# A two-layer encoder trunk on one core: products for the second layer's modulation are done later, the last heads' queries are copied at one point, the last head's operands are split in another order, and one query of the second layer is finished later

## The chip, the cores and the metric

The kernel runs on one core of a Trainium2 chip. The core has five engines, each with its own instruction stream that runs in order: TensorE (PE, matrix products), VectorE (DVE), ScalarE (ACT), GpSimd (POOL) and SyncE (SP), which in this kernel issues every DMA transfer. The metric is the device time of one execution in microseconds. One execution of each kernel is also recorded by the hardware profiler, and everything that is read of single instructions comes from that record.

## The reference

The input is a sequence of 1024 positions of width 1024 in float32, one batch. Two layers follow each other and a last RMS norm closes the trunk:

```python
for i in range(DEPTH):                       # DEPTH = 2
    shift, scale, gate = silu(c) @ ada_w[i] + ada_b[i], split in three
    h = rmsnorm(x, norm_g[i]) * (1.0 + scale) + shift
    y = diff_attention(h, ...) if i == 0 else mla(h, ...)
    x = x + gate * y
return rmsnorm(x, final_norm_g)
```

Layer 0 is differential attention with eight heads. One input projection gives q, k, v and z, each 1024 wide. q and k are turned by rotary position embedding (rope) in pieces of 64. For each head two attention maps are formed; the second is multiplied by a learned lambda and taken from the first, and the result meets the values. The head's output is normalised, multiplied by silu(z), and goes through an output projection.

```python
p = softmax(q @ k * scale)                   # two maps per head
p = p[:, :, 0] - lam * p[:, :, 1]
o = rmsnorm(p @ v, subln_g) * (1 - lambda_init) * silu(z)
y = o @ w_out
```

Layer 1 is latent attention: queries, keys and values come from narrow projections (384 and 256 wide). Each of its eight heads has 128 channels without rope, and 64 with it; the rope key is common to all heads.

## The kernel before

**Products.** Every matrix product of two float32 numbers is made of three reduced ones: each operand is split in a high part (a cast to the matrix engine's own float type) and a low part (the operand less its high part), and `mm3` (lines 181 to 184) adds high by high, high by low and low by high. So each tile of weights or activations goes through an ACT cast and a subtraction on DVE or POOL before PE can read it. Names show it: `wvr` is a value weight as loaded, `wvh` and `wvl` are its parts (L524, L533, L534); `wraw`, `wh`, `wl` (L206, L227, L228) are those of the other weights; `woh`, `wol`, `oah`, `oal` (L1177, L1178) those of layer 0's output projection. A matrix instruction is 128 x 128 by 128 x 512.

**Start of layer 0.** The tokens are normalised and transposed in two halves. The weights of the first 512 value channels meet both halves first (`vacc`). After that come the second half of head 0's keys and queries (`gen_half`, "half 1"), and then eight *value tiles* (`v0_tile`, sums in `vps`) for the other 512 channels, one for each 128 tokens. Each value tile ends in `store_v`: ACT casts the sum (L362), DVE subtracts (L363), and SP stores both parts to device memory (`vS`, L365), from where heads load them as `vt` (L374). Three `v_hl` buffers serve six of these stores.

**Modulation of layer 1.** The 2048 numbers of shift and scale of layer 1 are sixteen products of a 128 x 1024 weight with silu(c), each one instruction on DVE (`mod_dot`, L424) that waits for a 512 KB load (`ada<-in_ada_ss`, L419). `gen_mods` hands them out one at a time: seven in the first pass over the second half of the tokens, two in the second half of head 0's keys, two in that of its queries, and five among the value tiles, by the table `MODS`.

**Rope and queries.** For each half of a head's q or k, `rope` copies the sum to `rp_raw` on ACT (L321), swaps channel groups by four small transfers to `rp_sw` (L323), multiplies by cosine (`rp_r`, L324) and sine (L329), and adds both (`fin`, L331 on POOL or L336 on DVE). Then `g` stacks the result: `stack_q` makes two ACT casts (`qa`, L352, L353), two POOL subtractions (`qb`, L354, L355) and four transfers of 128 KB (L357, L358); `stack_k` makes `ks` likewise, with no transfers. These steps stand in a queue, `side`, and one of its entries is run at each tick while PE works at the stream of projections of the next heads; an entry `None` is a tick with nothing to do.

**Attention.** For each tile of 128 queries PE makes the two score maps `s` from `ks` and `qa`, `qb` (L851), DVE takes the maximum (`nm`, L400), ACT the exponential (`e`, L402), DVE combines both maps (L859), PE transposes (`tr`, L383), ACT and DVE split the transpose (`pth`, L385; `ptl`, L386), and PE multiplies it with the values (`pv`). The projections of the next heads (`acc`) and the gate z (`zth` by ACT at L785, `gz` by DVE at L786) are put between.

**Output projection of layer 0.** It is done on 512 x 512 blocks with seven products where the plain way takes eight (a scheme of Strassen's kind). Sums of blocks of the heads' outputs are formed by `combine` (four POOL instructions, L1124 to L1128), the operands are split by `split_a` and `split_w` (L1177, L1178), and the first products are begun during the last head's attention, by the table `PRE0`, with a step number `i` from 0 to 10. A block `k` is one that is kept in place; its loads are at L1313 and L1333.

**Layer 1.** The same order of work: value tiles (`vps`, `v_hl`), rope queries (`qpa`, `qpb`, by the same `stack_q`), score maps at L2003 and so on.

**Order.** Where the code asks for nothing else, a scheduler sets the order on each engine from the order of the code; `in_turn`, `behind` and `tc.issue_after` tie an instruction to a place behind another. Each engine then runs its list strictly in order, and so does SP: a transfer whose source isn't ready holds all that are behind it.

Of the kernel before, what the change touches and what calls it, by code (L numbers as in the profile page):

```python
# [42 lines left out]
SPL1 = 2  # L43
Z_PRE = 16
V_LATE = 6
MODS = (2, 1, 1, 1, 0, 0, 0, 0)
V1_AT = (3, 2)
NORM_AT = 5
PRE0 = (0, 0, 0, 0, 1, 2, 2, 2, 3, 2, 2)
PRE1 = (0, 0, 0, 0, 0, 0, 0, 1, 1, 1, 1)  # L50
LAST1 = (((0, 1), 0, HF), ((2,), 0, HF), ((3,), 0, 256), ((3,), 256, HF))
Z_LAST = 2
# [29 lines left out]
def trunk(ctx: ExitStack, tc: tile.TileContext, A, out):  # L82
# [447 lines left out]
    def split_wv(raw, eng=G):  # L530
        h_ = p1b.tile([P, HF], F32R, name="wvh", tag="wv", bufs=16)
        l_ = p1b.tile([P, HF], F32R, name="wvl", tag="wv", bufs=16)
        S.copy(h_, raw)  # L533
        eng.tensor_sub(l_, raw, f32v(h_))  # L534
        return h_, l_

    psum("ps1", accx=3, tr=1, cb=1)
# [183 lines left out]
    vacc = [bank("acc", "vacc") for _ in range(4)]  # L721
    for k in range(KT + SKEW1):
        if k < KT:
            if k > 0:
                next(mods_g)
            with tc.issue_after(q_split), tc.issue_after(q_mm):
                h_last = h_chunk(0, xs1, k, h0[k][1], p1, V if k in HL_V else G, k % 2 == 1)
        if k >= SKEW1:
            k0 = k - SKEW1
            hh, hl = h0[k0][1]  # L730
            for tt in range(4):
                c_ = slice(tt * P, (tt + 1) * P)
                mm3(vacc[tt], hh[:, c_], hl[:, c_], wv0[k0][0], wv0[k0][1], k0 == 0, k0 == KT - 1)
# [32 lines left out]
    def q_done(h):  # L766
        def f(acc, half):
            rot, fin = rope(wp, acc, half, SC0, *[G if h else V] * 2)

            def g():  # L770
                qa = a0a.tile([P, 2, HF], F32R, name="qa", tag="qs", bufs=4)
                qb = a0a.tile([P, 2, HF], F32R, name="qb", tag="qs", bufs=4)
                stack_q(qa, qb, r.pop() if r else fin())
                QS.setdefault(h, [None, None])[half] = qa, qb

            r = []
            sum_ = [lambda: r.append(fin()), None][: 1 + (h < 5)] if h else []
            side.add(*[None] * ROT, rot, *[None] * (DEF - 1 - ROT), *sum_, g)
        return f

# [23 lines left out]
        k_done(0)(kacc, 0)  # L804
    with tc.issue_after(mod_load.last):
        z0raw = fetch_strip([A["w_s0"][2, 0, f] for f in range(2)], [4, 4])
    for i, _ in enumerate(gen_half(wk0, h0, 1, lambda acc: k_done(0)(acc, 1))):
        if i % 4 == 3:
            next(mods_g)
    wz0 = split_strip(z0raw)  # L810
    q_done(0)(qacc, 0)
    for i, _ in enumerate(gen_half(wq0, h0, 1, lambda acc: q_done(0)(acc, 1))):
        if i % 4 == 3:
            next(mods_g)
    st1.close()
    st2a = ExitStack()
    a0a = pool(st2a, "a0a")
# [15 lines left out]

    pend = [t for t in side.q if t]
    side.q.clear()
    for t in pend[:4]:
        t()
    turn = 0
    stream0.step(Z_PRE)

# [431 lines left out]
    def extra0(i):  # L1272
# [41 lines left out]
        if i == 4:  # L1314
            sv.split_a(0, 0, G)
            both(0, 1)
            sv.split_a(0, 2, G)
        if i == 5:
            sv.split_w(0, 2)
        for n, h in ((), (), (), (), (), ((0, 3),), ((1, 0), (1, 1)), ((1, 2),), (), (), ())[i]:  # L1320
            both(n, h)
        while rests:
# [14 lines left out]
        if i == 8:  # L1337
            sv.split_w(1, 3)
            a11, a12, a21, a22 = k0["pair"]
            for n, t in ((2, a11), (3, a22), (4, a12), (5, a21)):  # L1340
                sv.kept[n][2] = t
            k0["sum"] = combine(*k0["pair"])
        if i > 7:
            next(k0["sum"], None)
        for _ in range(PRE0[i]):
            pre0.step()

# [83 lines left out]
            next(sp)  # L1431

    sv0.split_a(1, 3, G)
    e_last = mk["S"]
    assert pre0.n == 15
    for h in range(4):
# [501 lines left out]

    st5 = ExitStack()
    ap = pool(st5, "attn1")  # L1940
    KN, QN, QP, late_q = {}, {}, {}, []

    def kn_done(h):
        def f(acc, half):
# [14 lines left out]
    def qp_done(h):  # L1959
        def f(acc, half):  # L1960
# [8 lines left out]
            side.add(None, rot, *[None] * DEF1)  # L1969
            if h and half:  # L1970
                late_q.append(g)
            else:
                side.add(g)
        return f
# [92 lines left out]
    ap2 = pool(st5, "attn1b")  # L2067
    stp = ExitStack()
    ap3, nob = pool(stp, "attn1c", side="right"), 8
    for h in range(NH - 1):  # L2070
        attn1(h, lambda i: FILL1[i], lambda i: next(gate1, None))
        while late_q:
            late_q.pop(0)()
        stream1.step(sum(steps1[: h + 2]) - stream1.count)
# [308 lines left out]
```

## Time and profile before

| | |
|---|---|
| three runs, median (lowest to highest) | 1422.78 us (1421.39 to 1426.56) |
| the profiled execution | 1421.18 us |
| its span, first to last instruction | 1419.2 us |
| mean granted TensorE clock | 0.991 |
| busy: PE, DVE, ACT, POOL | 97%, 66%, 52%, 53% |

The profile's page gives, for each engine, the busy time as a share of the span. "Idle" of an instruction is the time its engine stood before it, and the name behind the arrow is what released it. Times inside the span count from its first instruction. An instruction's own length on PE is that of a pipelined product; two products of 512 columns that follow without a wait start 0.23 us apart.

### The profile page before, as it was taken

To read this page: it belongs to the slowest core of one execution; us is meant where nothing else is said; L and a number is where in the kernel's file an instruction comes from. 1 tells how busy PE (TensorE), PEld (TensorE's weight loads), DVE (VectorE), ACT (ScalarE), POOL (GpSimd) and SP (SyncE) were. 2 spreads that over 40 slices of the span, in tenths; PEclk is the share of its full clock that TensorE was granted. 3 is DMA by queue.
4 is the path that set the end of the run, shared out by engine and by line. 5 is a ranking of instruction groups with operands and counts; after the bars stand their busy time and mean duration, and the time that the engine had idled before them with its cause. 6 is when DMAs were issued, how large, how long until landed. Compare 5 with 4: busy or idle time off the path is not lost. (4 is left out here: it accounts for less than half of the span.)

```text
span 1419.2 us, 20732 instructions
## 1 busy us (share of the span) xinstructions
PE 1382.2 (97%) x7350; PEld 1152.0 (81%) x7350; DVE 939.5 (66%) x1339; ACT 736.9 (52%) x1331; POOL 752.1 (53%) x590
## 2 busy tenths in 40 slices
PE   8999999999999999999999999999999999999997
PEld 6777888888888887887787788887888888888886
DVE  8665677777666665668597885645666655555685
ACT  5523465565555655557546443335454454455554
POOL 5415174758686857575694323533141165653783
PEclk8999999999999999999999999999999999999999
DMA  9785734343444434426564136498544354566463
GB/s 344 250 231 182 221 93 134 99 136 98 149 114 154 135 117 120 141 75 193 163 231 163 38 104 216 129 313 223 167 114 129 94 176 171 188 208 209 142 243 119
DMA packets 149066, 231.54 MB, mean 163 GB/s; under 512 B 20577, under 2 KB 57569, under 8 KB 148962
## 3 DMA queue, kind: packets, MB, share of 16 engines
q1 hardware_dynamic: 148962, 230.21, 51.7%
q8 instruction: 58, 0.95, 0.3%
q14 instruction: 46, 0.38, 0.1%
HBM read 144.74 MB, written 61.81 MB: 146 GB/s over the span
## 5 line engine op out<-in xcount | busy, mean ns | idle before, releaser
L385 ACT CAST pth<-tr 128x512 fp32r<-128x512 f32 x256 | 150.1, 586 | 294.4 <-PE tr L383 292.4
L400 DVE TENSOR_REDUCE nm<-s 128x1 f32<-128x1024 f32 x192 | 233.7, 1218 | 90.6 <-PE s L851 78.8
L386 DVE TENSOR_TENSOR ptl<-tr,pth 128x512 fp32r<-128x512 f32 x256 | 176.0, 688 | 146.6 <-ACT pth L385 146.0
L228 POOL TENSOR_TENSOR wl<-wraw,wh 128x512 fp32r<-128x512 f32 (+2 forms) x79 | 101.4, 1285 | 197.8 <-ACT wh L227 166.3
L402 ACT ACTIVATE e<-s,nm 128x1024 f32<-128x1024 f32 x128 | 143.5, 1121 | 32.4 <-DVE nm L400 30.3
L383 PE MATMUL tr<-ident,e 128*128 128x128 f32 x1024 | 156.3, 275 | 3.0 <-DVE ptl L386 2.8
L383 PEld LDWEIGHTS tr<-ident,e 128*128 128x128 f32 x1024 | 122.0, 141 | 45.6 <-DVE ptl L386 21.0
L182 PE MATMUL acc<-h0h,wh 128*128 128x512 f32 x360 | 151.6, 421 | 0.0
L182 PE MATMUL pv<-pth,vt 128*128 128x256 f32 x512 | 147.1, 287 | 0.0
L183 PE MATMUL pv<-ptl,vt 128*128 128x256 f32 x512 | 145.7, 285 | 0.0
L184 PE MATMUL pv<-pth,vt 128*128 128x256 f32 x512 | 144.6, 282 | 0.0
L184 PE MATMUL acc<-h0h,wl 128*128 128x512 f32 x360 | 143.6, 399 | 0.0
L183 PE MATMUL acc<-h0l,wh 128*128 128x512 f32 x360 | 142.7, 396 | 0.0
L324 POOL TENSOR_TENSOR rp_r<-rp_raw,cosT 128x512 f32<-128x512 f32 x38 | 49.7, 1307 | 98.4 <-ACT rp_raw L321 49.8
L183 PEld LDWEIGHTS pv<-ptl,vt 128*128 128x128 f32 x512 | 97.6, 191 | 2.9
L182 PEld LDWEIGHTS pv<-pth,vt 128*128 128x128 f32 x512 | 97.5, 190 | 2.9
L184 PEld LDWEIGHTS pv<-pth,vt 128*128 128x128 f32 x512 | 97.6, 191 | 0.1
L1178 POOL TENSOR_TENSOR wol<-wol,woh 128x512 fp32r<-128x512 f32 x56 | 83.0, 1504 | 21.4 <-ACT woh L1177 18.8
L851 PE MATMUL s<-ks,qa 128*128 128x512 f32 x256 | 83.4, 407 | 6.3 <-DMA qa<-qa 4.5
L329 POOL TENSOR_TENSOR rp_sw<-rp_sw,sinT 128x512 f32<-128x512 f32 x42 | 56.3, 1340 | 52.7 <-DMA rp_sw<-rp_raw 52.1
L859 DVE SCALAR_TENSOR_TENSOR e<-s,z,e 128x1024 f32<-128x1024 f32 x64 | 82.2, 1284 | 2.2
L851 PE MATMUL s<-ks,qb 128*128 128x512 f32 x256 | 81.3, 398 | 0.8 <-DMA qb<-qb 0.8
(412 smaller groups left out, 3488.6 us busy)
## 6 DMA issues: line engine op xcount, KB each, us to landing
ada<-in_ada_ss SPq DMA_DIRECT2D x32, 512.0 KB, 5.6
wraw<-in_w_s SPq DMA_DIRECT2D x64, 256.0 KB, 2.9
vS<-v_hl SPq DMA_DIRECT2D x32, 512.0 KB, 5.8
vt<-vS SPq DMA_DIRECT2D x32, 512.0 KB, 4.8
wol<-tS SPq DMA_DIRECT2D x56, 256.0 KB, 5.0
tS<-ob SPq DMA_DIRECT2D x48, 256.0 KB, 2.0
rp_sw<-rp_raw SPq DMA_DIRECT2D x168, 64.0 KB, 2.0
bc_s<-bc_d SPq DMA_DIRECT2D x34, 256.0 KB, 4.0
```

What stands on the lines that cost most here:

```text
L182: PE.matmul(psum, ah, bh, start=first, stop=False, skip_group_check=skip)
L183: PE.matmul(psum, ah, bl, start=False, stop=False, skip_group_check=skip)
L184: mm3.last = PE.matmul(psum, al, bh, start=False, stop=last, skip_group_check=skip).ins
L228: sub = (V if pair_of else G).tensor_sub(l_[:, :n], raw[:, :n], f32v(h_[:, :n]))
L383: transpose_p.last = PE.transpose(tr[:, j, :], p[:, kt * P : (kt + 1) * P], ident).ins
L385: mk["S"] = S.copy(pth[kh][:, :, dst], tr).ins
L386: mk["V"] = V.tensor_sub(ptl[kh][:, :, dst], tr, f32v(pth[kh][:, :, dst])).ins
L400: mk["V"] = V.reduce_max(nm, s_ps, axis=AX.X, negate=True).ins
L402: mk["S"] = S.activation(e, s_ps, AF.Exp, bias=nm, scale=1.0, accum_out=zs).ins
L851: PE.matmul(s_ps[:, kc * HF : (kc + 1) * HF], src[:, c, ql], KS[h][kc][:, c, :], start=fst, stop=not fst)
L859: combined.append(V.scalar_tensor_tensor(out=e0, in0=e1, scalar=z1[:, 0:1], in1=e0, op0=ALU.mult, op1=ALU.add).ins)
L1178: sub = eng.tensor_sub(lo, raw, f32v(hi))
```

## The change

Four groups of edits, all of them to the order of work; no arithmetic is added or taken away.

1. *Modulation products.* Five of the sixteen `mod_dot` are moved. The first pass does six in place of seven, the second halves of head 0's keys and queries do none in place of four, and the value tiles do ten in place of five (`MODS`). Their loads move with them. The first four waiting tasks of `side` (among them the stacking of head 0's keys) are tied to a place behind the last split of a value weight.
2. *Queries of heads 5, 6 and 7.* The rope sum `fin` and the stacking `g`, which were one tick apart, are now one task, a tick earlier.
3. *Last head.* The split of weight block (0, 2) comes with its activation block, one of the early products moves from step 8 to step 7, and `combine`, which was done in steps 8 and 9, comes after the last split, `split_a(1, 3)`.
4. *Layer 1.* The stacking of the second half of head 0's rope query, which stood before the last value tiles, is done after tile 1 of the first head.

```diff
--- before.py
+++ after.py
@@ -43,10 +43,10 @@
 SPL1 = 2
 Z_PRE = 16
 V_LATE = 6
-MODS = (2, 1, 1, 1, 0, 0, 0, 0)
+MODS = (2, 3, 3, 2, 0, 0, 0, 0)
 V1_AT = (3, 2)
 NORM_AT = 5
-PRE0 = (0, 0, 0, 0, 1, 2, 2, 2, 3, 2, 2)
+PRE0 = (0, 0, 0, 0, 1, 2, 2, 3, 2, 2, 2)
 PRE1 = (0, 0, 0, 0, 0, 0, 0, 1, 1, 1, 1)
 LAST1 = (((0, 1), 0, HF), ((2,), 0, HF), ((3,), 0, 256), ((3,), 256, HF))
 Z_LAST = 2
@@ -531,7 +531,7 @@
         h_ = p1b.tile([P, HF], F32R, name="wvh", tag="wv", bufs=16)
         l_ = p1b.tile([P, HF], F32R, name="wvl", tag="wv", bufs=16)
         S.copy(h_, raw)
-        eng.tensor_sub(l_, raw, f32v(h_))
+        split_wv.last = eng.tensor_sub(l_, raw, f32v(h_)).ins
         return h_, l_
 
     psum("ps1", accx=3, tr=1, cb=1)
@@ -721,7 +721,7 @@
     vacc = [bank("acc", "vacc") for _ in range(4)]
     for k in range(KT + SKEW1):
         if k < KT:
-            if k > 0:
+            if 0 < k < 7:
                 next(mods_g)
             with tc.issue_after(q_split), tc.issue_after(q_mm):
                 h_last = h_chunk(0, xs1, k, h0[k][1], p1, V if k in HL_V else G, k % 2 == 1)
@@ -774,7 +774,7 @@
                 QS.setdefault(h, [None, None])[half] = qa, qb
 
             r = []
-            sum_ = [lambda: r.append(fin()), None][: 1 + (h < 5)] if h else []
+            sum_ = [lambda: r.append(fin()), None] if 0 < h < 5 else []
             side.add(*[None] * ROT, rot, *[None] * (DEF - 1 - ROT), *sum_, g)
         return f
 
@@ -804,14 +804,12 @@
         k_done(0)(kacc, 0)
     with tc.issue_after(mod_load.last):
         z0raw = fetch_strip([A["w_s0"][2, 0, f] for f in range(2)], [4, 4])
-    for i, _ in enumerate(gen_half(wk0, h0, 1, lambda acc: k_done(0)(acc, 1))):
-        if i % 4 == 3:
-            next(mods_g)
+    for _ in gen_half(wk0, h0, 1, lambda acc: k_done(0)(acc, 1)):
+        pass
     wz0 = split_strip(z0raw)
     q_done(0)(qacc, 0)
-    for i, _ in enumerate(gen_half(wq0, h0, 1, lambda acc: q_done(0)(acc, 1))):
-        if i % 4 == 3:
-            next(mods_g)
+    for _ in gen_half(wq0, h0, 1, lambda acc: q_done(0)(acc, 1)):
+        pass
     st1.close()
     st2a = ExitStack()
     a0a = pool(st2a, "a0a")
@@ -833,8 +831,9 @@
 
     pend = [t for t in side.q if t]
     side.q.clear()
-    for t in pend[:4]:
-        t()
+    with tc.issue_after(split_wv.last):
+        for t in pend[:4]:
+            t()
     turn = 0
     stream0.step(Z_PRE)
 
@@ -1314,9 +1313,7 @@
         if i == 4:
             sv.split_a(0, 0, G)
             both(0, 1)
-            sv.split_a(0, 2, G)
-        if i == 5:
-            sv.split_w(0, 2)
+            both(0, 2)
         for n, h in ((), (), (), (), (), ((0, 3),), ((1, 0), (1, 1)), ((1, 2),), (), (), ())[i]:
             both(n, h)
         while rests:
@@ -1339,9 +1336,6 @@
             a11, a12, a21, a22 = k0["pair"]
             for n, t in ((2, a11), (3, a22), (4, a12), (5, a21)):
                 sv.kept[n][2] = t
-            k0["sum"] = combine(*k0["pair"])
-        if i > 7:
-            next(k0["sum"], None)
         for _ in range(PRE0[i]):
             pre0.step()
 
@@ -1431,6 +1425,8 @@
             next(sp)
 
     sv0.split_a(1, 3, G)
+    for _ in combine(*k0["pair"]):
+        pass
     e_last = mk["S"]
     assert pre0.n == 15
     for h in range(4):
@@ -1938,7 +1934,7 @@
 
     st5 = ExitStack()
     ap = pool(st5, "attn1")
-    KN, QN, QP, late_q = {}, {}, {}, []
+    KN, QN, QP, late_q, first_q = {}, {}, {}, [], []
 
     def kn_done(h):
         def f(acc, half):
@@ -1969,6 +1965,8 @@
             side.add(None, rot, *[None] * DEF1)
             if h and half:
                 late_q.append(g)
+            elif half:
+                first_q.append(g)
             else:
                 side.add(g)
         return f
@@ -2067,8 +2065,13 @@
     ap2 = pool(st5, "attn1b")
     stp = ExitStack()
     ap3, nob = pool(stp, "attn1c", side="right"), 8
+    def amid1(i):
+        next(gate1, None)
+        if i and first_q:
+            first_q.pop()()
+
     for h in range(NH - 1):
-        attn1(h, lambda i: FILL1[i], lambda i: next(gate1, None))
+        attn1(h, lambda i: FILL1[i], amid1)
         while late_q:
             late_q.pop(0)()
         stream1.step(sum(steps1[: h + 2]) - stream1.count)
```

What stands where is shown at three places. Line numbers after the change are lower by one to four from L804 to L2066.

The first is DVE, around the last value weight splits (`wvl`) of the start of layer 0; `ISA ada,mod...` is a modulation product, and the row under it reads its sum. Before:

```order
L534 TENSOR_TENSOR wvl<-wvr,wvh 128x512 x2
L424 ISA ada,modb_105<-ada,c_202,vec 128x1024
L424 ISA modb_105 128x1
L324 TENSOR_TENSOR rp_r<-rp_raw,cosT 128x512
L534 TENSOR_TENSOR wvl<-wvr,wvh 128x512 x4
L336 TENSOR_TENSOR rp_r<-rp_r,rp_sw 128x512
L324 TENSOR_TENSOR rp_r<-rp_raw,cosT 128x512
L363 TENSOR_TENSOR v_hl<-vps,v_hl 128x512
L424 ISA ada,moda_104<-ada,c_202,vec 128x1024
```

and after:

```order
L534 TENSOR_TENSOR wvl<-wvr,wvh 128x512 x2
L324 TENSOR_TENSOR rp_r<-rp_raw,cosT 128x512
L534 TENSOR_TENSOR wvl<-wvr,wvh 128x512 x4
L324 TENSOR_TENSOR rp_r<-rp_raw,cosT 128x512
L336 TENSOR_TENSOR rp_r<-rp_r,rp_sw 128x512
L363 TENSOR_TENSOR v_hl<-vps,v_hl 128x512
L324 TENSOR_TENSOR rp_r<-rp_raw,cosT 128x512
L336 TENSOR_TENSOR rp_r<-rp_r,rp_sw 128x512
L324 TENSOR_TENSOR rp_r<-rp_raw,cosT 128x512
L786 SCALAR_TENSOR_TENSOR gz<-zth,acc 128x512
```

The product among the splits and the four behind them are gone from here, and the gate `gz` follows directly; before, it came behind another `v_hl` and the sums for lambda.

The second is SP while PE ends head 5's attention and goes on to head 6, whose first query half is `qa`, `qb`; `rp_sw` belongs to head 6's second query half, and `bc_s` is a row that is spread over all partitions for the normalisation of a finished head. Before:

```order
L408 DMA bc_d<-rq_y 128x4
L206 DMA wraw<-in_w_s 128x512
L323 DMA rp_sw<-rp_raw 32x512 x2
L410 DMA bc_s<-bc_d 128x512
L323 DMA rp_sw<-rp_raw 32x512 x2
L357 DMA qa<-qa 64x512
L358 DMA qa<-qa 64x512
L357 DMA qb<-qb 64x512
L358 DMA qb<-qb 64x512
```

and after:

```order
L408 DMA bc_d<-rq_y 128x4
L357 DMA qa<-qa 64x512
L206 DMA wraw<-in_w_s 128x512
L358 DMA qa<-qa 64x512
L410 DMA bc_s<-bc_d 128x512
L357 DMA qb<-qb 64x512
L358 DMA qb<-qb 64x512
L323 DMA rp_sw<-rp_raw 32x512 x4
```

The two transfers of `qa` now stand ahead of the spread row, those of `qb` right behind it, and the four small ones of `rp_sw` behind them all.

The third is POOL in the last head's attention, where the operands of the output projection are split; `ob<-ob` are the four instructions of `combine`. Before:

```order
L1178 TENSOR_TENSOR wol<-wol,woh 128x512 x2
L1124 TENSOR_TENSOR ob<-ob 128x512
L1125 TENSOR_TENSOR ob<-ob 128x512
L1127 TENSOR_TENSOR ob<-ob 128x512
L1128 TENSOR_TENSOR ob<-ob 128x512
L1178 TENSOR_TENSOR oal<-k_6673,oah 128x512
```

and after:

```order
L1177 TENSOR_TENSOR wol<-wol,woh 128x512 x2
L1177 TENSOR_TENSOR oal<-k_6673,oah 128x512
L1123 TENSOR_TENSOR ob<-ob 128x512
L1124 TENSOR_TENSOR ob<-ob 128x512
L1126 TENSOR_TENSOR ob<-ob 128x512
L1127 TENSOR_TENSOR ob<-ob 128x512
```

The low part `oal` of the kept block is now made ahead of `combine`. In layer 1, on SP, the four transfers of the second rope query half (`qpa`, `qpb`) move behind five stores `vS` and two loads `c2h`; on ACT its two casts move behind all the value tiles' casts.

## The prediction

> **What bounds the kernel now.** I read the page first. It has TensorE busy for nearly the whole span, in 1421.18 us for the profiled execution:
>
> ```profile
> span 1419.2 us, 20732 instructions
> PE 1382.2 (97%) x7350; PEld 1152.0 (81%) x7350; DVE 939.5 (66%) x1339; ACT 736.9 (52%) x1331; POOL 752.1 (53%) x590
> ```
>
> No product is taken away, so only PE's idle time and time at a lowered clock can be won: 37 us of idle. Second I read PE's waits (line waited for, total us, times, longest):
>
> ```profile
> PE s L851 <- DMA qa<-qa: 4.5, 4, 2.3
> PE vps L182 <- DVE v_hl L363: 2.3, 1, 2.3
> PE oy L184 <- POOL oal L1178: 1.7, 2, 1.2
> PE oy L183 <- POOL wol L1178: 1.7, 3, 1.1
> PE vps L182 <- DVE gz L786: 1.5, 1, 1.5
> PE vps L183 <- DVE wvl L534: 1.0, 1, 1.0
> PE s L851 <- DMA qb<-qb: 0.8, 2, 0.5
> ```
>
> Nearly all of them are at places that the change touches. Third, stretches of the span: length, busy us (and count) of PE, PEld, DVE, ACT, POOL, then granted clock, DMA share, GB/s.
>
> ```profile
> 80.00:98.00 18.00, 17.01 (x74) 13.40 (x73) 10.68 (x17) 4.24 (x8) 0.00 (x0) 1.00 0.88 268
> 98.00:108.00 10.00, 8.40 (x28) 5.79 (x27) 6.78 (x8) 3.56 (x6) 4.36 (x4) 0.83 0.90 228
> 114.00:144.00 30.00, 28.52 (x126) 23.23 (x126) 14.19 (x24) 10.90 (x18) 16.69 (x11) 1.00 0.60 182
> 120.00:132.00 12.00, 10.52 (x47) 8.35 (x46) 7.54 (x15) 6.72 (x12) 10.89 (x7) 1.00 0.16 57
> 558.00:566.00 8.00, 5.74 (x24) 4.40 (x23) 2.71 (x4) 0.87 (x2) 4.06 (x3) 0.79 0.42 106
> 676.00:680.00 4.00, 3.40 (x11) 2.78 (x12) 3.04 (x5) 1.62 (x3) 3.99 (x4) 0.64 0.00 0
> 968.00:974.00 6.00, 3.65 (x17) 2.68 (x16) 2.42 (x3) 3.57 (x7) 3.43 (x3) 1.00 0.92 263
> ```
>
> Three of PE's waits are followed by time at a lowered clock (0.83, 0.79, 0.64), so these cost more than the wait itself; the longest, at 969, is not.
>
> **A. Modulation products.** The value tiles stop between 98 and 108: 10.00 less 8.40 is 1.6 us idle, and 10 us at 0.83 lose up to 1.7 us. PE waits there for the splits of the last value weights, whose loads are held back by full DMA queues (share 0.88). Taking one product ahead of them away takes one load of 512 KB away: at the row's 268 GB/s that is 2.0 us of transfer, and its DVE instruction 1.3 us. The loads then come up to 2.0 us earlier; of the 3.3 us that can be won I take 1.3, since the remaining loads keep their own order and buffers. Ends: 0 and 3.0.
>
> The wait for `gz` is a chain that I read in the order of time on ACT and DVE:
>
> ```profile
> 119.47 0.59 ACT L362 CAST v_hl<-vps 128x512 fp32r<-128x512 f32 x1 [8.64 <-PE vps L184]
> 119.96 0.62 ACT L344 CAST ks<-rp_r 64x512 fp32r<-64x512 f32 x1
> 123.41 0.69 DVE L324 TENSOR_TENSOR rp_r<-rp_raw,cosT 128x512 f32<-128x512 f32 x1 [2.62 <-POOL ks L347]
> ```
>
> The key casts stood behind a value tile's cast, POOL's `ks` behind them, DVE's `rp_r` behind that, and `gz` behind `rp_r`. In the new order the casts, `rp_r` and `gz` come ahead of this tile. ACT stood idle for 8.64 us before it, which holds four casts of 0.62, so the 1.5 us go, and 0.1 of refilling: 1.6 (ends 0 and 1.6).
>
> Against it stand five products and five loads in the value tiles. A product is 1.28 us, and up to 2.36:
>
> ```profile
> L424 DVE CUSTOM_DVE_ANT_0 ada<-ada,c,vec x16: 1272/1283/2360, 71.8 to 148.9; 128x1024 f32<-128x1024 f32 x16
> 110.07 2.36 DVE L424 CUSTOM_DVE_ANT_0 ada<-ada,c,vec 128x1024 f32<-128x1024 f32 x1
> 110.06 1.29 POOL L329 TENSOR_TENSOR rp_sw<-rp_sw,sinT 128x512 f32<-128x512 f32 x1 [0.63 <-DMA rp_sw<-rp_raw]
> ```
>
> So DVE gets 6.4 to 11.8 us more. It is idle for 15.8 of the 30 us from 114 to 144 (30 less 14.19), and the DMA engines are nearly empty from 120 to 132 (share 0.16), room for twelve times 0.84 by 268 GB/s, 2.7 MB, where five loads are 2.6 MB. The cover is thin but there. What could break it is SP's order:
>
> ```profile
> SPq L206 <- POOL wl L228: 12.2, 2, 11.0
> ACT v_hl L362 <- DMA vS<-v_hl: 10.7, 2, 5.4
> ```
>
> SP already stands 11 us for a weight buffer with stores `vS` behind it, and ACT then waits twice for a store to land, 10.7 us, while PE's idle time in these 30 us (30 less 28.52) is the 1.5 for `gz` and nothing else. In the new order the first of these stores goes ahead of that stand, so loads may slip by about 5 us unnoticed. I take 0.7 of loss (ends 0 and 3). A comes to 1.3 + 1.6 - 0.7 = 2.2.
>
> [...]
>
> **B. Queries.** In time order, ACT and SP ahead of head 6, PE, and, last, PE at head 7:
>
> ```profile
> 554.18 0.61 ACT L352 CAST qa<-rp_r 64x512 fp32r<-64x512 f32 x1
> 555.29 1.14 SPq L323 DMA_DIRECT2D rp_sw<-rp_raw  x2
> 556.53 0.54 SPq L357 DMA_DIRECT2D qa<-qa  x1
> 560.86 0.58 PE L851 MATMUL s<-ks,qa 128*128 128x512 f32 x1 [2.26 <-DMA qa<-qa]
> 561.66 0.63 PE L182 MATMUL acc<-h0h,wh 128*128 128x512 f32 x1
> 562.09 0.63 PE L183 MATMUL acc<-h0l,wh 128*128 128x512 f32 x1
> 632.59 0.70 PE L851 MATMUL s<-ks,qa 128*128 128x512 f32 x2 [1.20 <-DMA qa<-qa]
> ```
>
> Now the casts come a tick earlier, ahead of an exponential, and `qa` goes out ahead of `bc_s` and `rp_sw`: about 3 us earlier, which covers 2.26. `qb` still stands behind `bc_s`; if it lands 0.3 to 1.3 us late, that is a new, smaller wait. Behind the old wait products start 0.43 us apart (561.66, 562.09) where 0.23 is usual, for some seven of them: 1.3 us. Of 2.3 + 1.3 = 3.6 I take 2.9 (ends 0.9 and 3.6). Of the other waits for `qa` (4.5 less 2.3) and `qb` (0.8), head 7 has 1.2 and heads 4 and 5 share 1.8. Head 4 is not changed; I give head 5 a third, 0.6, which goes. At head 7 the order puts `qa` ahead of only two of four `rp_sw`, at 0.6 us each, but its casts later: 0 (ends -1.2 and 1.2). B: 3.5.
>
> **C. Last head.**
>
> ```profile
> 674.04 1.29 POOL L923 TENSOR_TENSOR o<-o,gz 128x512 f32<-128x512 f32 x1 [3.34 <-ACT o L917]
> 694.26 1.29 POOL L1124 TENSOR_TENSOR ob<-ob 128x512 f32<-128x512 f32 x1
> 699.62 1.26 POOL L1178 TENSOR_TENSOR oal<-k,oah 128x512 fp32r<-128x512 f32 x1
> ```
>
> `wol` of block (0, 2) stood behind the product with `gz`, which waited 3.34 us for ACT; it now goes ahead, and the 1.1 go, with the clock's 0.36 of 4 us behind it (1.4): I take 2.4 (ends 0 and 2.5). `oal` started 5.4 us behind the first `combine` instruction (699.62 less 694.26) and PE waited 1.2 for it; ahead of them it is early by far, and `combine` itself ends one instruction (1.3 us) later, which nothing waits for before the next group: 1.2 (ends 0 and 1.2). One weight load goes out behind five others, and a POOL product of head 7 behind two rope steps: 0.4 of loss, ends 0 and 1.5. C: 3.2.
>
> **D. Layer 1.**
>
> ```profile
> 968.94 0.62 ACT L352 CAST qpa<-rp_r 64x512 fp32r<-64x512 f32 x1 [3.41 <-POOL rp_r L331]
> 970.22 1.07 ACT L362 CAST v_hl<-vps 128x512 fp32r<-128x512 f32 x2
> 987.28 0.63 PE L2003 MATMUL s<-kps,qpa 128*128 128x512 f32 x2
> 978.98 2.32 SPq L1862 DMA_DIRECT2D c2h<-in_c  x2
> DMA to landing us min/median/max: 7.2/7.6/8.0
> ```
>
> ACT stood 3.41 us for POOL's sum with a finished value tile behind it. Without the two casts there PE's 2.3 for `v_hl` go, and 0.2 of refilling: 2.5. New is a late query: its four transfers now follow the `c2h` loads (issued from 979.0, landing in 7.2 to 8.0 us), and PE wants it at 987.28, less the 2.5 won: 984.8. The queue is ahead by as much and by four transfers, so the query lands between 984 and 987: 0.7 of loss (ends 0 and 2.3). D: 1.8.
>
> **Sum.** 2.2 + 3.5 + 3.2 + 1.8 = 10.7. Against the profiled 1421.18 that is 1410.5; the median of the runs is 1.6 above it, so 1412 for the median. All best ends give 1.6 + 3.0 + 0.6 + 3.6 + 1.2 + 2.5 + 1.2 + 2.5 = 16.2, so 1406.6; all worst ends 0 - 3 + 0.9 + 0.6 - 1.2 - 1.5 + 0.2 = -4.0, so 1427, if everything failed at once. What this kernel's measurement can tell from no change is about 0.5%, 7.1 us: the line is at 1415.7, and my forecast 3.7 us beyond it.
>
> The clock is worth 1.3 + 1.3 in this sum. [...]
>
> **Rivals.** *Waits that move.* The late operand is replaced by the next one: `qb` behind `bc_s` at head 6, the value weights at 99, the late query at 985. With A at 0.3, B at 1.5, C at 2.4 and D at 0.5 the gain is 4.7: 1418, no difference. For it speaks that these engines had little to spare (`qa` and `qb` were issued within 2 us of each other); against it, that C and the `gz` wait leave nothing late behind them.
>
> *Slower: SP stands among the value tiles.* SP issues the new loads three at a time ahead of a store `vS`, and there are three buffers, so a third load waits for a product, with stores and queries behind it. Fully in a row, five products in their long form (11.8) and five transfers of 2.0 us (10) are 21.8 us; with the gain of A's rest, B, C and D (11.4, without the 0.7) that gives 1433. It turns the sign once PE waits over 11.4 us there, and shows as slower over 18.5. Against it: 15.8 us of idle DVE, the empty DMA stretch, and no PE wait there now.
>
> *The lowered clock stays.* If the clock falls after whatever short waits remain, at head 6 and in the last head, the 1.3 + 1.3 are not won: 1412 + 2.6 = 1414.7, hardly past the line. That it stayed at 1.00 behind the wait at 969 says that the link is loose.
>
> *The change doesn't do what it says.* "Last heads' queries at once" holds for heads 5 and 6 by the order, for head 7 half; without B's 2.9 the time is 1415, at the line.
>
> **Chances.** Forecast (faster) 0.52; the clock stays 0.08, of it 0.05 faster; B failing, at the line, 0.05, of it 0.03 faster; waits that move, no difference, 0.26; slower by the value tiles 0.09. So faster 0.60, same 0.31, slower 0.09. The range reaches from all best ends, 1406, into the slow rival's beginning, 1424.
>
> **What would show it.** Right: no PE wait for `gz` near 124, none for `qa` near 556, none for `oal` near 697, none for `v_hl` near 967; granted clock 1.00 near 560 and 676; PE's idle sum down from 37 us to about 29. Wrong: new PE waits for `v_hl` or `nm` between 110 and 150, for `qpa` or `qpb` near 985, or for `qb` near 556.

## The result, and the profile after

| | before | changed |
|---|---|---|
| median of six runs each, us | 1421.62 | 1413.83 |
| lowest to highest | 1418.34 to 1426.56 | 1411.87 to 1415.68 |
| profiled execution, its span | 1421.18, 1419.2 | 1415.68, 1414.0 |
| granted clock in the profiled execution | 0.991 | 0.992 |

The ratio is 0.9943, with a 95% interval of 0.9922 to 0.9963: 8 us faster, between 5 and 11. A second series of six runs of the changed kernel (last batch below) has a median of 1411.52 and a ratio of 0.9927 (0.9913 to 0.9942). The prediction said 1412, of 1406 to 1424.

First the page of the changed kernel, then PE's waits (line waited for, total us, times, longest), those that answer to the waits shown before:

```profile
span 1414.0 us, 20751 instructions
PE 1379.2 (98%) x7350; PEld 1150.3 (81%) x7350; DVE 939.8 (66%) x1339; ACT 737.5 (52%) x1331; POOL 752.8 (53%) x590
```

```profile
PE tr L383 <- DVE ptl L386: 5.1, 7, 1.5
PE s L850 <- DVE e L858: 2.7, 5, 1.0
...
PE s L850 <- DMA qa<-qa: 1.8, 2, 1.4
...
PE s L850 <- DMA qb<-qb: 1.5, 2, 0.9
PE vps L182 <- ACT wvh L533: 1.4, 1, 1.4
...
PE vps L183 <- DVE wvl L534: 0.8, 1, 0.8
```

The waits for `gz` (1.5), for `v_hl` in layer 1 (2.3) and the long one for `qa` (2.3) are gone. The two for the value weights are still there, 1.4 and 0.8 where 0.5 and 1.0 stood. The waits for `ptl` and `e`, ACT and DVE inside attention, were there before, 4.5 us together:

```profile
PE tr L383 <- DVE ptl L386: 2.8, 5, 0.9
...
PE s L851 <- DVE e L859: 1.7, 3, 1.0
```

They grew to 7.8. PE's idle time went from 37.0 us to 34.8 (1414.0 less 1379.2); the prediction had named 29 as a sign. So 3.0 of the 5.2 us between the two spans are busy time that got shorter. The mean clock, 0.991 and 0.992, accounts for some 1.4 of that by an estimate (0.001 of 1414); the rest stays open.

Stretches of the changed kernel (length, busy us of PE, PEld, DVE, ACT, POOL, then clock, DMA share, GB/s):

```profile
98.00:108.00 10.00, 8.37 (x22) 6.11 (x23) 4.37 (x6) 5.19 (x9) 7.00 (x6) 0.66 0.45 126
114.00:150.00 36.00, 36.00 (x160) 29.78 (x160) 23.61 (x39) 8.99 (x16) 13.60 (x8) 1.00 0.98 305
555.00:566.00 11.00, 10.46 (x62) 8.80 (x61) 6.60 (x9) 5.29 (x10) 7.11 (x6) 1.00 0.39 107
676.00:684.00 8.00, 7.58 (x49) 6.49 (x48) 7.26 (x11) 6.89 (x13) 5.25 (x6) 1.00 0.49 123
```

With ten products among the value tiles PE does not wait there at all (36.00 of 36), though the DMA engines are full (0.98). The stall at 98 to 108 is as long as before (1.63 us idle, 1.60 before) and at a lower clock, 0.66 where it was 0.83. The clock at head 6 and in the last head is full (1.00 from 555 to 566 and from 676 to 684).

To compare more than two traces I cut the span at instructions that every kernel has: the first product of head 0's second query half (`acc`, near 82), the first maximum `nm` of heads 1, 4 and layer 1's head 2, two `nm` inside heads 5 and 6, the first output product `oy`, the first `oz`, and the first value product `vps` of layer 1 ("layer 1's start"). A time in the next table is the start of one such instruction less that of another, taken from the trace of each kernel.

### The profile page after: what moved, and what is told of

Read it like the earlier page. It is cut to its first block, busy times and chain, and to the rows that moved or that the text cites. A ratio compares the mean times of both kernels' runs of the same rounds, so it can differ in the third digit from the quotient of the medians.

```text
span 1414.0 us, 20751 instructions
## 1 busy us (share of the span) xinstructions
PE 1379.2 (98%) x7350; PEld 1150.3 (81%) x7350; DVE 939.8 (66%) x1339; ACT 737.5 (52%) x1331; POOL 752.8 (53%) x590
## 4 chain that ended last, share of the span: by engine, by line
PE 78%; DVE 8%; DMA 4%; POOL 4%; ACT 3%; issue 2%; SPq 1%; POOLq 0%; DVEq 0%; ACTq 0%
PE s L2001 10%; PE acc L184 8%; PE acc L182 8%; PE acc L183 8%; PE tr L383 7%; PE s L850 6%; PE pv L184 4%; PE pv L182 4%; PE pv L183 4%; PE vps L183 1%; PE vps L184 1%; PE vps L182 1%; PE zacc L184 1%; PE zacc L183 1%; PE zacc L182 1%
```

## The experiments

Each kernel stands against the kernel before on the same chip. For e1 to e4 each kernel has one part of the change alone; the lines name the edits, which are those of the change:

```diff
 e1 (A):  MODS = (2, 3, 3, 2, ...); if 0 < k < 7; no next(mods_g) in head 0's halves;
          with tc.issue_after(split_wv.last): pend[:4]
 e2 (B):  sum_ = [lambda: r.append(fin()), None] if 0 < h < 5 else []
 e3 (C):  PRE0, both(0, 2) at i == 4, combine after split_a(1, 3)
 e4 (D):  first_q, amid1
```

> Part A alone (five modulation products moved, key tasks behind the last value split). Theory of the prediction: 2.2 us less than before: the wait for gz near 124 gone (1.6), the stall at 98 to 108 shortened by 1.3, 0.7 lost in the value tiles. Rival, from the first pair of traces: the stall at 97 to 107 keeps its full size, because the last value weights are issued when a buffer comes free and not when the queue empties; then only the 1.6 for gz are won, and the stall with its lowered clock is as dear as before (3.7 us) or dearer (5 us), so 0.4 to 1.6 us less than before.

> Part B alone (queries of heads 5 to 7 one tick earlier). Theory of the prediction: 3.5 us less: head 6's wait for qa and its lowered clock cost 3.7 us and leave at most 0.7 for qb; head 5 wins 0.6; head 7 stays. Rival, from the first pair of traces: head 6 wins 3.0, but head 5 loses about what it had (a new wait for the difference e or for ptl takes the place of the one for qa), so 1.5 to 2.5 us less in all.

> Part C alone (last head's splits, combine later). Theory of the prediction: 3.2 us less, kept to the end. Rival: PE's waits for wol near 675 and oal near 700 go (2.7 us at the end of the last head's attention), but the output projection behind it, where DVE runs without a gap for about 30 us, hands up to 1.3 us back, as PE's wait for x (0.4 us before, 1.6 in the changed kernel) says: 1.5 us less at the start of layer 1.

> Part D alone (late rope query of layer 1). Theory of the prediction: 1.8 us less: PE's 2.35 us for v_hl near 969 gone, and a wait of about 0.7 for the late query at tile 4 of the first head. Rival, from the first pair of traces: no wait for the query at all, but waits for the split ptl in the first tiles, because the query's two casts now stand among the exponentials on ACT: 1.2 us near 984; the sum is the same, 1.8, and the place of the loss tells the two apart.

| kernel | median us (runs) | ratio to before (95%) |
|---|---|---|
| e1, A alone | 1420.41 (12) | 0.9988 (0.9975 to 1.0001) |
| e2, B alone | 1420.86 (11) | 0.999 (0.998 to 1.0) |
| e3, C alone | 1419.16 (12) | 0.9975 (0.9964 to 0.9986) |
| e4, D alone | 1417.71 (6) | 0.9971 (0.996 to 0.9982) |

The times alone tell C and D, but not A and B, from no change. The parts' ratios add up to -0.0076, the whole has -0.0057 and -0.0073. The stages of the traces tell more, since each part can be compared over all kernels that have it or don't (mean, lowest to highest, us):

| stage | parts without it | with it | won | predicted |
|---|---|---|---|---|
| A: 82 to head 1 | 131.69 (130.67 to 132.40), 5 traces | 129.76 (128.32 to 131.29), 5 | 1.9 | 2.2 |
| B: head 4 to a tile inside head 5 | 107.77 (107.26 to 108.46), 5 | 108.51 (108.41 to 108.69), 8 | -0.7 | 0.6 |
| B: to the middle of head 6 | 68.40 (67.12 to 69.55), 5 | 66.05 (65.87 to 66.36), 8 | 2.4 | 2.9 |
| B: to the first `oy` (head 7) | 67.24 (67.08 to 67.42), 5 | 67.71 (67.40 to 67.92), 8 | -0.5 | 0 |
| C: first `oy` to first `oz` | 43.33 (43.07 to 43.63), 5 | 40.33 (40.31 to 40.34), 9 | 3.0 | 3.2 |
| D: layer 1's start to head 2 | 129.03 (128.33 to 130.20), 5 | 125.96 (125.50 to 126.76), 8 | 3.1 | 1.8 |
| sum | | | 9.2 | 10.7 |

**A.** The wait for `gz` was 1.5 us in all five traces without A and is in none with it. PE's idle time in the value tiles is 0. The stall near 100 did not get shorter: PE's waits for `wvh` and `wvl` between 92 and 106 add up to 1.3 to 2.4 us in the five traces without A, and to 1.3 to 2.2 with it. The clock behind it was even lowered more often: from 98 to 108 it is below 1.00 in one of the five traces without A (0.83) and in four of the five with it (0.66, and 0.83 three times). Ten us at 0.83 lose up to 1.7, so by this estimate the clock took some 1.7 us of the mean with A and 0.3 of the mean without, and with them 1.4 of what A's order had won. Whether A's order brings this on, or chance, five traces can't tell. The rival held.

**B.** Alone it is within its error of nothing, less than either expectation; by the stages head 5 and head 7 give back half of what head 6 wins. ACT at head 5 in the changed kernel (second trace), and PE behind it:

```profile
478.54 0.62 ACT L352 CAST qa<-rp_r 64x512 fp32r<-64x512 f32 x1 [2.08 <-POOL rp_r L331]
479.19 0.62 ACT L353 CAST qa<-rp_r 64x512 fp32r<-64x512 f32 x1
479.83 0.60 ACT L321 ACTIVATE rp_raw<-acc 128x512 f32<-128x512 f32 x1
480.32 0.58 ACT L385 CAST pth<-tr 128x512 fp32r<-128x512 f32 x1
...
491.03 0.62 ACT L352 CAST qa<-rp_r 64x512 fp32r<-64x512 f32 x1 [1.69 <-POOL rp_r L331]
491.67 0.62 ACT L353 CAST qa<-rp_r 64x512 fp32r<-64x512 f32 x1
492.32 1.12 ACT L402 ACTIVATE e<-s,nm 128x1024 f32<-128x1024 f32 x1
```

```profile
481.69 0.55 PE L383 MATMUL tr<-ident,e 128*128 128x128 f32 x3 [0.79 <-DVE ptl L386]
```

and ACT at the same place before:

```profile
481.03 0.62 ACT L352 CAST qa<-rp_r 64x512 fp32r<-64x512 f32 x1 [1.58 <-POOL rp_r L331]
481.68 0.62 ACT L353 CAST qa<-rp_r 64x512 fp32r<-64x512 f32 x1
482.32 0.58 ACT L385 CAST pth<-tr 128x512 fp32r<-128x512 f32 x1
```

A tick earlier puts the copy `rp_raw` ahead of `pth`, and, for the other half, lets ACT stand for POOL's sum with an exponential behind it, where before the exponential went first (492.24, with the casts at 493.34). The query is early, and the softmax late: all eight traces with B have 0.7 us for `e` and 0.8 for `ptl` in this stage. At head 7 no wait accounts for the 0.5; PE's idle time there grew by 0.1 only.

**C.** 3.0 us in a stage that varies by 0.03 us with it: the predicted size, but not from the predicted terms. Some of PE's waits from 664 to 708, before and with C alone:

```profile
PE oy L183 <- POOL wol L1178: 1.1, 1, 1.1
PE tr L383 <- DVE ptl L386: 0.9, 1, 0.9
```

```profile
PE tr L383 <- DVE ptl L386: 2.6, 3, 1.5
PE oy L184 <- POOL oal L1178: 0.5, 1, 0.5
```

The wait for `wol` goes, of the 1.7 for `oal` 0.5 is left, and the waits for `ptl` grow. PE's idle time in the stage is 3.9 to 4.6 us without C and 3.1 with it, 1.2 less in the mean. The rest, by an estimate, is the clock: from 660 to 706 it is 0.96 in all five traces without C and 1.00 in all nine with it, and 46 us at 0.96 lose some 1.8. In the kernel before it fell behind the wait of 1.1 us for `wol`, near 677 and in e9 near 673; in e1, e2 and e4 behind one of 2.2 to 2.4 us for `ptl`, near 687 to 691. The 1.2 us that my rival had seen handed back in the output projection come with or without C (below, e9). The rival falls.

**D.** The wait for `v_hl` is gone, none for the late query appears. The 3.1 us are more than the 1.8 of both expectations. PE's waits from 960 to 1000 in the changed kernel:

```profile
PE tr L383 <- DVE ptl L386: 1.3, 2, 1.1
```

The place was named by the rival; 0.4 in D alone and 0.5 in the second trace of the changed kernel (e10) say that it is not a fixed price.

The second batch asks what held the value weights, what head 5 is worth, and how late the query may be. Each line is an edit of the changed kernel, with what stood there behind the `#`.

```diff
 e5:  raw = p1b.tile([P, HF], F32, name="wvr", tag="wvr", bufs=3)        # 2
 e6:  if 0 < k < 5:              MODS = (2, 4, 4, 2, ...)                # 7; (2, 3, 3, 2)
 e7:  sum_ = [...] if 0 < h < 6 else []                                  # 0 < h < 5
 e8:  if i > 1 and first_q:                                              # if i and first_q
```

> The changed kernel with three buffers in place of two for a loaded value weight (wvr). Theory of the buffers: the last value weights are late because their loads wait for the split of the one two places earlier; with one more buffer they are issued some 5 us earlier, PE's waits for them between 95 and 104 (2.2 to 3.0 us, and up to 1.9 of lowered clock) shrink below 1 us, and the kernel is 2 to 3 us faster than the changed one. Rival, the theory of the prediction: the loads are late because the DMA queues are full of other transfers at 80 to 98; a third buffer then only makes them wait longer in the queue, and the waits stay within 0.5 us of what they were.

> The changed kernel with two more modulation products moved out of the first pass into the value tiles (four left there, twelve in the value tiles). Theory of the prediction (less traffic and less DVE work ahead of the last value weights): the waits between 95 and 104 shrink by 2 us or more, since the two products at 83 and 87 stand ahead of two of the value splits on DVE; the two more products in the value tiles cost nothing. Rival (order of buffers alone): SP is held at 83 to 88 by the stores of the finished values, so the loads behind them leave at the same time as before, and the waits stay at 2 to 3 us. Second question: PE idles between 114 and 150 if twelve products are more than the value tiles can hide (0 us with ten).

> The changed kernel with head 5's queries put back to the old order (only heads 6 and 7 are changed). Theory from the traces: at head 5 the earlier copy removes a wait for qa and qb of 0.9 us but brings waits for ptl and e of 1.4 near 482 and 498; put back, PE loses 1.4 there in place of 1.9, so 0.5 us less than the changed kernel, and head 6 keeps its 3 us. Rival (the prediction: head 5 gains 0.6): 0.6 us more than the changed kernel.

> The changed kernel with the late query of layer 1 finished one tile later (after tile 2 of the first head in place of tile 1). Theory of the prediction (the query lands just in time for tile 4): one tile is 2.9 us, so PE waits 2 to 3 us for qpa at tile 4. Rival (the query has slack, and the waits for ptl near 980 come from its casts among the exponentials): no wait for qpa, and the 1.2 us near 980 move to the next tile or go.

| kernel | median us (runs) | ratio to before (95%) |
|---|---|---|
| e5, three buffers | 1415.89 (6) | 0.9947 (0.9932 to 0.9962) |
| e6, four products ahead | 1412.66 (5) | 0.9929 (0.9915 to 0.9943) |
| e7, head 5 as before | 1414.89 (6) | 0.9948 (0.9932 to 0.9963) |
| e8, query a tile later | 1413.39 (5) | 0.9936 (0.9923 to 0.9949) |

**What held the value weights.** PE's waits from 75 to 110 with three buffers (e5), and from 75 to 165 with four products ahead (e6):

```profile
PE acc L182 <- DVE v_hl L363: 2.3, 1, 2.3
PE acc L184 <- POOL wl L228: 0.4, 1, 0.4
```

```profile
PE s L850 <- DVE e L858: 1.0, 1, 1.0
PE acc L184 <- POOL wl L228: 0.4, 1, 0.4
PE acc L182 <- DVE v_hl L363: 0.4, 1, 0.4
```

In both the waits for `wvh` and `wvl` are gone, but for reasons that must be told apart. In the changed kernel the last two value weights leave at 95.6 and 96.2, each as soon as a split on DVE has freed one of the two buffers (these two splits end at 95.5 and 96.1), and their last split ends at 101.3. With a third buffer the last three leave between 88.7 and 91.1, so it was the buffer that held them. Landing then takes longer (5.8 and 4.9 us for the first two of them, where the last two took 2.6 and 2.8), and their last split ends at 97.7. But the scheduler also moved work ahead; PE lost 2.3 us for `v_hl` (until 85.0) and came to the value tiles 3.1 us later, which by itself would have covered most of the old waits, 2.2 us together. So nothing was won, where 2 to 3 us were expected.

With four products it is the first splits that come earlier. DVE in the changed kernel, then in e6:

```profile
86.74 1.28 DVE L424 CUSTOM_DVE_ANT_0 ada<-ada,c,vec 128x1024 f32<-128x1024 f32 x1 [1.75 <-DMA ada<-in_ada_ss]
...
87.95 1.29 DVE L534 TENSOR_TENSOR wvl<-wvr,wvh 128x512 fp32r<-128x512 f32 x2
...
98.81 2.47 DVE L534 TENSOR_TENSOR wvl<-wvr,wvh 128x512 fp32r<-128x512 f32 x2 [2.67 <-ACT wvh L533]
```

```profile
82.91 1.29 DVE L363 TENSOR_TENSOR v_hl<-vacc,v_hl 128x512 fp32r<-128x512 f32 x2 [0.46 <-ACT v_hl L362]
84.12 1.80 DVE L534 TENSOR_TENSOR wvl<-wvr,wvh 128x512 fp32r<-128x512 f32 x2
...
98.87 1.64 DVE L534 TENSOR_TENSOR wvl<-wvr,wvh 128x512 fp32r<-128x512 f32 x1 [1.40 <-ACT wvh L533]
```

In the changed kernel the split waits behind a product that itself stands 1.75 us for its load; without it the splits come 3.8 us earlier (84.12 for 87.95), and SP's next two weight loads went out from 85.6 in place of 88.7. The product that the change took away stood behind these splits, so it could free no buffer earlier. But the last split ends only 0.8 us earlier (100.5 for 101.3). What took the wait away in e6 is another order on PE, which the scheduler chose: 48 products `acc` come after the first 5 of the value tiles, where the changed kernel has 28 of these ahead, and the next value product starts at 106.1. The cleaner test is e11, below. Twelve products in the value tiles, on the other hand, are too many: PE waits 1.0 us for `e` of the first score, whose maximum stands right behind two products on DVE (143.15 to 145.77).

**Head 5.** Put back, PE waits 2.9 us for `qa`:

```profile
PE s L850 <- DMA qa<-qa: 2.9, 1, 2.9
PE tr L383 <- DVE ptl L386: 0.3, 1, 0.3
```

SP shows why, in e7 and then before:

```profile
483.49 0.34 SPq L410 DMA_DIRECT2D bc_s<-bc_d  x1
483.94 0.50 SPq L357 DMA_DIRECT2D qa<-qa  x1
```

```profile
485.78 0.53 SPq L357 DMA_DIRECT2D qa<-qa  x1
...
488.29 0.58 SPq L410 DMA_DIRECT2D bc_s<-bc_d  x1
```

Before, head 5's `qa` went out ahead of the spread row `bc_s`; in e7 it stands behind it, as head 6's did, and lands 5.0 us after its issue (at 488.92) in place of 3.0. So putting back one edit did not give back the old order. What it does show is that the waits in the softmax belong to the earlier copy: of 0.7 for `e` and 0.8 for `ptl` only 0.3 is left. Both expectations were wrong in size: the stage took 111.3 us, against 108.5 in the changed kernel and 107.8 before. The median shows no difference from the changed kernel that its interval would bear.

**The late query.** One tile later there is still no wait for it, but PE waits 1.6 us for values `vt`, which were not waited for in D alone or in the changed kernel:

```profile
980.13 0.39 PE L182 MATMUL pv<-pth,vt 128*128 128x256 f32 x1 [1.58 <-DMA vt<-vS]
```

The query's transfers stand between two loads of `vt` on SP there; that they hold the second was not tried apart. The query had slack, against the expected wait of 2 to 3 us, and the 0.7 us that I had charged were not owed.

The last batch repeats both kernels, and looks for a better number of products.

```diff
 e9:   the kernel before, unchanged
 e10:  the changed kernel, unchanged
 e11:  if 0 < k < 6:             MODS = (2, 4, 3, 2, ...)
 e12:  as e6
```

> The kernel before, once more, to see what of the differences between traces comes back by itself. Theory (PE's waits are set by the order, the lowered clock behind them is chance): the waits of the first trace return within 0.5 us at the same places (2.3 for qa at head 6, 2.35 for v_hl near 969, 1.5 for gz, 1.1 and 1.2 in the last head), while the granted clock behind them (0.83, 0.79, 0.64 in the first trace) comes out different. Rival (clock and wait belong together, as the sum of the prediction has it): the clock is lowered again behind the same three waits.

> The changed kernel once more, on the same chip as the next two. The same two theories: the waits near 97 to 102 (2.2 us), at head 7 (1.4) and near 754 (1.6) return; the 0.66 of granted clock behind the first, and the 1.07 for ptl near 980, need not. Ratio to the kernel before 0.994, within 0.002.

> The changed kernel with one more modulation product moved from the first pass into the value tiles (five and eleven). If the last value weights are late because their buffers come free behind modulation products on DVE, the waits near 97 to 102 lie between those with six products ahead (1.6 to 2.2 us) and with four (none): about 1 us or less; and the wait of 1.0 us at 152 that twelve products in the value tiles brought is not there. That is 1 to 2 us less than the changed kernel. Rival (only the two products directly ahead of a split count): no change against the changed kernel.

> Four products in the first pass and twelve in the value tiles, once more, beside the changed kernel on one chip: 2 us less than the changed kernel (waits near 97 to 102 gone, 2.2, and their lowered clock; 1.0 lost at 152). Rival: the gain seen before was chance in the clock, and both agree within 1 us.

| kernel | median us (runs) | ratio to before (95%) |
|---|---|---|
| e9, before again | 1420.86 (1) | |
| e10, changed again | 1411.52 (6) | 0.9927 (0.9913 to 0.9942) |
| e11, five products ahead | 1408.47 (5) | 0.9909 (0.9894 to 0.9924) |
| e12, four products again | 1411.21 (5) | 0.9924 (0.991 to 0.9937) |

**Before again.** Stretches of e9:

```profile
98.00:108.00 10.00, 8.71 (x36) 6.08 (x35) 6.67 (x8) 3.56 (x6) 4.61 (x4) 1.00 0.79 231
555.00:566.00 11.00, 9.63 (x55) 8.10 (x54) 5.98 (x9) 4.66 (x9) 5.83 (x5) 1.00 0.40 120
676.00:684.00 8.00, 8.00 (x51) 7.08 (x50) 6.96 (x9) 6.25 (x12) 4.16 (x5) 0.96 0.43 122
966.00:976.00 10.00, 7.64 (x27) 5.79 (x27) 3.81 (x5) 4.69 (x8) 3.33 (x3) 0.83 0.98 289
```

and three of its waits:

```profile
PE s L851 <- DMA qa<-qa: 3.8, 4, 1.4
...
PE vps L182 <- DVE v_hl L363: 2.4, 1, 2.4
...
PE oy L182 <- DVE x L1404: 1.6, 1, 1.6
```

The waits come back at their places; only head 6's is 1.4 where it was 2.3, more than the 0.5 us that were allowed for. The clock comes back in part. It is full at 98 to 108 and at head 6, where it was 0.83 and 0.84 over the same stretches, and 0.83 behind the wait for `v_hl`, where it was 1.00. In the last head it fell again behind the wait for `wol`, some 4 us earlier in the span, so that only its end lies in the third row (0.96). So one trace doesn't tell behind which waits the clock falls, but it isn't all chance either: in the last head it fell in every trace without C.

And the 1.6 us for `x` in the output projection stands here in the kernel before too: its 0.4 in the first trace was the exception (the stage takes 52.9 us in two traces, 53.2 in one and 54.1 to 54.2 in eleven); without it the first two spans would lie some 1.2 us further apart.

**Changed again.** In e10 the ratio and the waits came as expected: 2.0 us for the value weights, 1.2 at head 7, 1.6 for `x`. The clock behind the first was 0.83, where it was 0.66, and the waits for `ptl` near 980 came to 0.5. PE's idle time was 32.6 us, against 38.1 in e9.

**Five products.** PE's waits from 75 to 165:

```profile
PE acc L184 <- POOL wl L228: 0.7, 1, 0.7
PE acc L182 <- DVE v_hl L363: 0.2, 1, 0.2
```

Neither the value weights nor the first score are waited for. The product that stood 1.75 us ahead of the splits is gone; the four loads leave 3.4 to 3.5 us earlier than in the changed kernel (from 85.1 and from 92.1), and the last split ends at 96.8 in place of 101.3. Here too PE's order is another, with 14 products of the value tiles ahead of the 48 `acc`; but in the old order the first product that needs the seventh weight would have come at 96.3 (eighteen products of 0.23 us behind 92.2, an estimate), when its split, begun at 95.5, was done. So the product ahead of the splits held the weights, as far as one trace can show it. The stage took 126.8 us, against 129.9 in e10 and 127.8 with four; the median is some 3 us below the changed kernel's on the same chip (runs 1407.66 to 1411.63 against 1410.47 to 1413.53). That is more than the 1 to 2 us expected, and against the rival, no change. It is the fastest kernel here, 0.9909 of the kernel before. e12 gained 2.1 us against e10 in this stage, but in the median only 0.3; the gain of four products over six is not shown.

## Why the prediction was right

The time, 1413.83 and in the second series 1411.52, lies around the predicted 1412, and the sum by stages is 9.2 us where I had 10.7. The parts are less even than the sum, and that it came so near is in part luck: D won 1.3 us more than its price and B 2.3 less, and C has its size by other terms.

- **The stall near 100, 1.3 predicted, no shortening measured.** The step that failed is "whose loads are held back by full DMA queues ... the loads then come up to 2.0 us earlier". They left 0.3 to 0.7 us earlier. In the changed kernel they wait for one of two buffers, which a split on DVE frees (the last two leave at 95.6 and 96.2, behind splits that end at 95.5 and 96.1); the product taken away stood behind the first of those splits. The landing did take longer for the first two of the four (5.5 and 5.1 us, against 2.6 and 2.8), but the buffer held the issue. e11, without the product ahead of the splits, had its loads 3.4 us earlier and no such wait.
- **`gz`, 1.6 predicted, a wait of 1.5 gone.** It was there in every trace without A and in none with it. The loss in the value tiles, 0.7 predicted, was 0 with ten products and 1.0 with twelve (0.8 in e12). The DMA stretch from 120 to 132 was empty before (share 0.16) and took the loads (0.95).
- **B, 3.5 predicted, 1.2 measured.** Head 6 was right in mechanism (2.4 for 2.9, and of the expected wait for `qb` of 0.3 to 1.3 there is 0.5 in one trace, 0.2 or less in the others); 0.7 of its 2.4 is the clock, by an estimate from the two of five traces without B in which it fell (0.84 from 555 to 566, where 11 us lose some 1.8). Head 5 had the wrong sign: I counted the wait for the query that would go and not what the two casts would push back on ACT, and I gave its 0.6 no worse end. At head 7, costed at 0, it lost 0.5.
- **C, 3.2 predicted, 3.0 measured**, and steady. But I had 1.9 us of waits and 1.3 of clock, and it was 1.2 of idle time and some 1.8 of clock: the growing wait for `ptl` was in no term.
- **D, 1.8 predicted, 3.1 measured.** 2.5 for the casts was right (2.4 against the three traces without D in which the clock stayed full); the late query's 0.7 was not charged by the chip, and e8 shows it had a tile to spare. Another 0.7, by an estimate, is the clock, which fell behind the old wait in two of five traces without D (0.83 from 966 to 976 in e3 and e9), where the stage took some 1.7 us more.
- **The clock, 2.6 us of the sum.** I tied it to two of the three places where the one trace showed it. Over all traces it fell at head 6 in two of five without B (0.84), in the last head in five of five without C (0.96 from 660 to 706), behind `v_hl` in two of five without D (0.83), and in none with these parts (1.00); at the stall near 100 in one of five without A (0.83) and in four of five with it (0.66, and 0.83 three times). What was won is the chance of it at the first and third place, and nearly the whole of it at the second; at the stall it was lost.
- **The signs.** The waits for `gz`, for `qa` at head 6, for `oal` near 697 and for `v_hl` went, and the clock near 560 and 676 was full. PE's idle time did not fall to 29 us but to 34.8 and 32.6: waits for `ptl` and `e` grew where the others went.
- The rivals: waits that move came true for head 5 and in the last head, too little to decide. SP's stand among the value tiles did not come (PE busy for 36.00 of 36). No run shows five products of 2.36 us each: of the ten in the value tiles in the first trace of the changed kernel one took 2.30 us, three 1.59 to 1.78, and six 1.27 to 1.28.

## What to carry to other kernels

PE's waits, here 0.5 us for `wvh` and 1.0 for `wvl` behind a DMA share of 0.88, did not tell whether a load was late behind a full queue or for want of a buffer; ask which instruction frees the buffer, and what stands ahead of it. When an experiment makes a wait go, look whether the waiting engine still comes to that place at the same time and in the same order. When a step is moved earlier on an engine that runs in order, count what it pushes back there (at head 5, 0.7 us for `e` and 0.8 for `ptl`), with its own wait for its input, as well as what it serves. And one trace showed the waits of an order well, but not which of them the clock would follow (behind 2.35 us for `v_hl` it was 1.00, behind 2.4 in the second trace 0.83): take a second trace of the same kernel before the clock enters a sum.

## What the runs showed of the hardware that was not expected

The granted clock fell behind a wait as short as 1.1 us (for `wol`; 0.64 from 676 to 680 in the first trace of before) and stayed full behind one of 2.35 us (for `v_hl`; 1.00 from 968 to 974 in the same trace), and in a second trace of the same kernel fell in part behind others (e9: 0.83 from 966 to 976, behind 2.4 us for `v_hl`, and 1.00 from 98 to 108, where it had been 0.83); a fall lasted 3.4 us at half the clock (0.50 from 561.1 to 564.5 in the first trace of before), and twice that, 6.8 us, at the stall in the first trace of the changed kernel (0.50 from 100.5 to 107.3); over the six executions of the changed kernel the mean clock went from 0.992 to 0.998, with times 3.8 us apart (1415.68 and 1411.87). In the output projection DVE and POOL run without a pause (both busy for 20.00 of 20 us from 726 to 746 in the first trace of before), and two subtractions of one kind take 2.38 us in the first trace of before and 3.52 in the second trace of the changed kernel:

```profile
742.99 2.38 DVE L1178 TENSOR_TENSOR oal<-oal,oah 128x512 fp32r<-128x512 f32 x2
```

```profile
735.81 3.52 DVE L1177 TENSOR_TENSOR oal<-oal,oah 128x512 fp32r<-128x512 f32 x2
```

That 1.1 us is nearly all of the difference between the two lengths of the stage. In both, POOL works beside them: its subtraction for `wol` starts within 0.02 us of them and takes 1.85 us in the first and 1.28 in the second, so the engine that is short in one is long in the other. Why now the one and now the other is long was not shown: no run here tries it apart.
